# A convolution and MLP block on one core: features made between the units of the second projection, the last residual moved into the MLP, own tiles for passing loads, chunk loads by groups, another end

## The chip, the core and the metric

One core of a Trainium2 chip runs the whole kernel. TensorE (PE) multiplies; VectorE (DVE), ScalarE (ACT) and GpSimd (POOL) work on rows; SyncE (SP) issues DMAs, and so do POOL's and ACT's own queues. The metric is device time in microseconds (us) of one execution.

## The reference

One layer over 2048 tokens of width 1024. Its mixer is a short gated convolution, followed by a squared-ReLU MLP. Both parts have a root mean square norm ahead and behind.

```
a = modulate(rmsnorm(x, g_pre), shift1, scale1)
b, c, v = split(a @ sc_w_in, 3)
y = (b * depthwise_conv3(c * v, sc_conv)) @ sc_w_out
h = x + gate1 * rmsnorm(y, g_post)
m = modulate(rmsnorm(h, g_pre_ff), shift2, scale2)
f = square(relu(m @ w_in)) @ w_out          # w_in 1024x4096, w_out 4096x1024
out = h + gate2 * rmsnorm(f, g_post_ff)
```

The six rows of shifts, scales and gates come from silu(c) @ ada_w + ada_b.

## The kernel before

**Numbers.** All tensors are float32. Each operand of a large product is kept as a high and a low part of a shorter type (F32R), made by a cast on ScalarE and a subtraction on VectorE (`split`, L135), and each product is three matmuls of 128x128 by 128x512 (high by high, high by low, low by high). Features lie on the partitions, tokens along the free axis, 512 to a block; there are four blocks q = 0 to 3, and two pairs of blocks s = 0, 1. A tile of SBUF is [128, 2, 512] float32, 512 KB.

**Stages.** `conv_in(q)` multiplies by w_sci and gates; `conv_out(q)` (L312) multiplies by w_sco. It has 8 units j of 24 matmuls; behind each unit ScalarE copies the sums out of PSUM (y[j], L320), squares them (`ssy.add`), and behind all of them come the norm's rows (`rows`, L183), then the residual: x is loaded again (xr, L325), scaled y is added to it (L328, L329), the result goes to DRAM (h_buf, on POOL's queue, L331), and its squares give the rows of the next norm (rh). After conv_in(3) come m_of(0), conv_out(2) and conv_out(3). `m_of(s)` (L335) makes the MLP's input for a pair: for each of 8 k it loads h (hm, SP's queue), scales it on VectorE (L342), takes the high part on ScalarE (L343) and the low part on VectorE (L344). For each s there follow 16 steps of `hidden` (four chunks ch of the 4096 inner features, kp = 0 to 3; four groups of 24 matmuls each, then ReLU and square). The second MLP product is one level of a seven-product scheme for 2x2 blocks (`PRODUCTS`, L33), so `features` (L351) makes 7 tiles of sums and differences per hidden step and SP writes them to DRAM (h_store). Then come 16 units of `product` (L442), each 7 products m0 to m6 of 12 matmuls, adding into f tiles; the unit's first-time results are copied by ScalarE (L459), the others added by VectorE (L461). Each chunk needs 28 h tiles, loaded on POOL's queue (`load_hidden`, L393, issue at L400), for four units. `finish(s)` (L497) takes the norm of f, scales it, adds h and stores the output: for s = 0 in steps beside the hidden steps of s = 1, for s = 1 at the end.

**Order.** A scheduler (Tile) orders each engine's instructions ahead of the run by priority, which is the order in which the program emits them, except inside `tc.high_priority()`. Tiles of one tag are a ring: in the instruction list of this kernel, buffers of a tag are handed out in the order in which the program first writes its tiles, so a tile emitted later gets its buffer after all those emitted ahead of it. The tag ts has 41 tiles and serves nearly everything: y, m, hm, xr, h, f, e. The weights have tags of their own (wf 4 tiles raw, wr 7 split). Each waiting instruction holds what stands behind it on its engine or queue.

Of the kernel before, what the change touches and what calls it, by code (L numbers as in the profile page):

```python
# [9 lines left out]
F32 = mybir.dt.float32  # L10
# [5 lines left out]
D = 1024  # L16
# [23 lines left out]
def conv_block_kernel(ctx: ExitStack, tc: tile.TileContext, xt, c, cols, ada, w_first, w_sci, w_sco, w_in, w_out,  # L40
# [12 lines left out]
    def pair(name, tag="ts", dtype=F32):  # L53
        return sbuf([P, 2, TB], dtype, tag, bufs[tag], name)
# [50 lines left out]
    xt0 = [load(xt[0, i], f"xt0_{i}") for i in range(KT // 2)]  # L105
    cols_sb = const.tile([P, 13, KT], F32, name="cols_sb")
    nc.sync.dma_start(cols_sb, cols)
    gain_sb, adab_sb, convw_sb = cols_sb[:, 0:4], cols_sb[:, 4:10], cols_sb[:, 10:13]
# [200 lines left out]
                next(background, None)  # L309
            gate(q, j, *ps)  # L310

    def conv_out(q):  # L312

        g = [parts.pop((q, k)) for k in range(KT)]
        y, ssy = y_tiles(f"y{q}"), RootMean(f"ry{q}")
        for j in range(KT):
            w = load_weights(w_sco[j], f"wo{q}_{j}")
            ps = acc_bank(f"y{q}_{j}_ps")
            project(w, g, ps)
            nc.scalar.copy(y[j], ps)  # L320
            ssy.add(y[j])
        r = ssy.rows()
        ssh = RootMean(f"rh{q}")
        for i in range(KT // 2):
            xr = load(xt[q, i], f"xr{q}_{i}")  # L325
            for s in range(2):
                j = 2 * i + s
                nc.vector.scalar_tensor_tensor(y[j], y[j], G2[:, j:j + 1], r, op0=ALU.mult, op1=ALU.mult)  # L328
                nc.vector.tensor_add(xr[:, s], y[j], xr[:, s])  # L329
                ssh.add(xr[:, s])  # L330
                nc.gpsimd.dma_start(h_buf[q // 2][j][:, q % 2], xr[:, s])  # L331
        nc.gpsimd.dma_start(r_buf[q // 2][:, q % 2], ssh.rows())


    def m_of(s):  # L335

        r = load(r_buf[s], f"r2_{s}")
        res = []
# [7 lines left out]
        return res  # L346
# [4 lines left out]
    def features(y, name, to):  # L351

        y0, y2, y3 = y
        y1 = pair(f"{name}_y1")
# [31 lines left out]
    def one(res, name, t):  # L386
        res[name] = t[:, 0], t[:, 1]

    def two(res, names, tiles):
        for i, n in enumerate(names):  # L390
            res[n] = tuple(t[:, i] for t in tiles)

    def load_hidden(s, ch):  # L393

        tiles = [[None] * 7 for _ in range(KP)]
        for group in ((0,), (1, 2), (3, 4), (5, 6)):
            for kp in range(KP):
                for i in group:
                    t = tiles[kp][i] = pair(f"h{kp}_{i}", "ts", F32R)
                    nc.gpsimd.dma_start(t, h_store[s][ch][kp][i].bitcast(F32R))  # L400
        sets = []
        for x in tiles:
            res = {}
            one(res, "11", x[0])
            for i, names in enumerate((("T1", "T2"), ("21", "T3"), ("22", "T4"))):
                two(res, names, x[1 + 2 * i:3 + 2 * i])
            sets.append(res)
        return sets

    def lone(src, name, tag):  # L410
        t = pair(name, tag, F32R)
# [53 lines left out]
    class PairRootMean:  # L465
# [3 lines left out]
            self.name, self.acc, self.eps = name, None, EPS * D / P  # L469

        def add(self, x):
            sq = pair(f"{self.name}_sq")
            nc.scalar.activation(sq, x, AF.Square)
            if self.acc is None:
                self.acc = sq
            elif self.eps:
                nc.vector.scalar_tensor_tensor(self.acc, sq, self.eps, self.acc, op0=ALU.add, op1=ALU.add)
                self.eps = 0
            else:
                nc.vector.tensor_add(self.acc, self.acc, sq)  # L480

        def rows(self):
# [9 lines left out]
                nc.vector.scalar_tensor_tensor(r[:, i], v[:, i], 1.5, r[:, i], op0=ALU.add, op1=ALU.mult)  # L492
            return r

    f_buf = [dram_pair(f"fb{k}") for k in range(KT)]

    def finish(s, f, ss):  # L497
        r = ss.rows()
        for k in range(KT):
            h = load(h_buf[s][k], f"hr{s}_{k}")  # L500
            t = f[k] if s else load(f_buf[k], f"fr{k}")
            nc.vector.scalar_tensor_tensor(t, t, G5[:, k:k + 1], r, op0=ALU.mult, op1=ALU.mult)
            nc.vector.tensor_add(h, t, h)
            nc.sync.dma_start(out[s, k], h)
            yield


    def x_rows(q):
        ss = RootMean(f"rx{q}")
        for i in range(KT // 2):  # L510
            t = load(xt[q, i], f"xs{q}_{i}")
            for h in range(2):
                ss.add(t[:, h])
        return ss.rows()

    def a_of(q, r):
        res = []
        for i in range(KT // 2):
            t = load(xt[q, i], f"xt{q}_{i}")
# [3 lines left out]
        return res  # L523

    later = {}
    background = (s for m in (2, 3, 4, 5) for s in mod_rest(m))
# [33 lines left out]
    for q in range(1, NB):  # L560
        a = a1
        conv_in(q, a, range(4))
        if q < NB - 1:
            r = x_rows(q + 1)
        conv_in(q, a, range(4, 8))
        if q < NB - 1:
            a1 = a_of(q + 1, r)
        else:
            for j in range(KT):
                gate_split(q, j)  # L570
            later["m"] = m_of(0)
        for _ in background:
            pass
        conv_out(q - 1)
    conv_out(NB - 1)

    def run_makers(makers, i, then):
        def between(m):
            if m == 1 and then:
# [7 lines left out]
    rest = iter(())  # L587
    for s in range(NS):
        for ch in range(NCH):
            for kp in range(KP):  # L590
                if s and (ch, kp) == (0, 2):
                    rest = finish(0, f, ss)
                hidden(s, ch, kp, later["m"])
                if (ch, kp) > (1, 0):
                    next(rest, None)
        for _ in rest:
            pass
        units = [(ch, jp) for ch in range(NCH) for jp in range(KP)]
        ws = [{} for _ in units]
# [4 lines left out]
        later["h"] = load_hidden(s, 0)  # L604
        f, ss = [pair(f"f{s}_{j}") for j in range(KT)], PairRootMean(f"rf{s}")

        def fetch():
            if ch < NCH - 1:
                later["h"] = load_hidden(s, ch + 1)
            elif s < NS - 1:  # L610
                later["m"] = m_of(s + 1)

        for i, (ch, jp) in enumerate(units):
            h = later["h"]
            js = jp, jp + KP
            e = [f[j] for j in js]
            product(ws[i], h, e, f"f{s}_{ch}_{jp}", ch > 0, run_makers(makers, i, fetch if jp == KP - 1 else None))
            if ch == NCH - 1:
                for j in js:
                    ss.add(f[j])  # L620
                    if s == 0:
                        nc.sync.dma_start(f_buf[j], f[j])
    for _ in finish(NS - 1, f, ss):
        pass


_INS = ["xt", "c", "cols", "ada", "w_first", "w_sci", "w_sco", "w_in", "w_out"]

# [47 lines left out]
```

## Time and profile before

| what | us |
|---|---|
| median of three runs | 2176.29 (2174.86 to 2179.14) |
| the profiled execution | 2179.44 |
| its span (first to last instruction) | 2177.7 |
| PE busy in it | 2057.7 |
| last matmul of the last product starts | 2142.24 |

The profiled execution is one of its own, not one of the three. Its span leaves out what lies before the first and after the last instruction. The page's mean granted clock of PE over the span is 0.973 of full speed (2.4 GHz). A line such as `PE y_ps L153 <- ACT y L320` says that PE waited, ahead of the matmuls of line 153 into y_ps, for ScalarE's instruction of line 320; "x" counts instructions.

### The profile page before, as it was taken

To read this page: it belongs to the slowest core of one execution; us is meant where nothing else is said; L and a number is where in the kernel's file an instruction comes from. 1 tells how busy PE (TensorE), PEld (TensorE's weight loads), DVE (VectorE), ACT (ScalarE), POOL (GpSimd) and SP (SyncE) were. 2 spreads that over 40 slices of the span, in tenths; PEclk is the share of its full clock that TensorE was granted. 3 is DMA by queue.
4 is the path that set the end of the run, shared out by engine and by line. 5 is a ranking of instruction groups with operands and counts; after the bars stand their busy time and mean duration, and the time that the engine had idled before them with its cause. 6 is when DMAs were issued, how large, how long until landed. Compare 5 with 4: busy or idle time off the path is not lost.

```text
span 2177.7 us, 23307 instructions
## 1 busy us (share of the span) xinstructions
PE 2057.7 (94%) x8880; PEld 1683.0 (77%) x8880; DVE 1257.4 (58%) x1691; ACT 784.1 (36%) x1026; POOL 158.2 (7%) x272
## 2 busy tenths in 40 slices
PE   6799999999999789999998999998999999999993
PEld 3587888888888567888886888886888887788882
DVE  6768765865756666343444466575455554455666
ACT  3233334334433435444443212134444444221221
POOL 2000000000000000000012211200000002112100
PEclk7999999999999899999999999999999999999997
DMA  6565633433424347555579756754658789779533
GB/s 223 183 213 200 204 136 136 172 132 136 171 100 145 125 140 263 224 211 224 212 260 377 274 182 249 270 181 157 261 215 297 282 296 352 247 272 317 187 133 154
DMA packets 127696, 463.48 MB, mean 213 GB/s; under 512 B 14561, under 2 KB 14561, under 8 KB 127585
## 3 DMA queue, kind: packets, MB, share of 16 engines
q1 hardware_dynamic: 92448, 335.11, 42.7%
q0 software_dynamic: 35136, 126.89, 16.3%
q8 instruction: 69, 1.13, 0.2%
q14 instruction: 43, 0.34, 0.0%
HBM read 322.49 MB, written 139.46 MB: 212 GB/s over the span
## 4 chain that ended last, share of the span: by engine, by line
PE 83%; DMA 6%; DVE 4%; issue 3%; ACT 1%; POOL 1%; SPq 0%; DVEq 0%; POOLq 0%; ACTq 0%
PE hid L153 29%; PE c L153 20%; PE f_a L454 14%; PE y_ps L153 8%; PE f_b L454 7%; PE f_c L454 3%; DMA hs<-h_lo 1%; PE c L552 1%; DMA ada<-in_ada_dram 1%; DMA adar<-in_ada_dram 1%; DMA hm<-hb 1%; DMA h<-hs 1%; POOL h L400 1%; DMA xr<-in_xt_dram 1%; DVE ada L230 0%
## 5 line engine op out<-in xcount | busy, mean ns | idle before, releaser
L153 PE MATMUL c<-a_parts,wc_hi 128*128 128x512 f32 x1440 | 444.6, 390 | 0.7 <-ACT a_parts L219 0.7
L153 PE MATMUL hid<-m_hi,wi_hi 128*128 128x512 f32 x1024 | 395.2, 392 | 8.9 <-ACT m_hi L343 7.8
L153 PE MATMUL hid<-m_lo,wi_hi 128*128 128x512 f32 x1024 | 399.6, 390 | 0.0
L153 PE MATMUL hid<-m_hi,wi_lo 128*128 128x512 f32 x1024 | 399.4, 390 | 0.0
L153 PEld LDWEIGHTS c<-a_parts,wc_hi 128*128 128x128 f32 x1440 | 271.1, 188 | 57.7 <-ACT a_parts L219 1.1
L153 PE MATMUL c<-a_parts,wc_lo 128*128 128x512 f32 x720 | 280.7, 390 | 3.4 <-DVE wc_lo L137 3.4
L137 DVE TENSOR_TENSOR wi_lo<-wi,wi_hi 128x1024 fp32r<-128x1024 f32 x64 | 78.3, 1224 | 286.1 <-PE hid L153 280.6
L153 PEld LDWEIGHTS hid<-m_hi,wi_hi 128*128 128x128 f32 x1024 | 193.4, 189 | 51.3 <-ACT m_hi L343 9.5
L153 PEld LDWEIGHTS hid<-m_lo,wi_hi 128*128 128x128 f32 x1024 | 193.1, 189 | 40.3
L153 PEld LDWEIGHTS hid<-m_hi,wi_lo 128*128 128x128 f32 x1024 | 192.9, 188 | 40.2
L400 POOL DMA_DIRECT2D h<-hs x224 | 121.2, 541 | 1119.9 <-DMA hs<-h_lo 411.6
L153 PE MATMUL y_ps<-gs,wo_hi 128*128 128x512 f32 x512 | 160.4, 395 | 17.2 <-ACT y L320 17.2
L454 PE MATMUL f_a<-h,wf_s_hi 128*128 128x512 f32 x512 | 163.4, 394 | 10.7 <-ACT f L459 10.7
L454 PE MATMUL f_b<-h,wf_s_hi 128*128 128x512 f32 x512 | 166.8, 394 | 1.4 <-DMA h<-hs 1.1
L153 PEld LDWEIGHTS c<-a_parts,wc_lo 128*128 128x128 f32 x720 | 135.5, 188 | 31.9 <-DVE wc_lo L137 3.9
L137 DVE TENSOR_TENSOR wc_lo<-wc_raw,wc_hi 128x1024 fp32r<-128x1024 f32 x90 | 109.9, 1222 | 82.0 <-PE c L153 47.8
L381 ACT ACTIVATE e<-hid 128x512 f32<-128x512 f32 x128 | 75.2, 596 | 227.4 <-PE hid L153 227.4
L137 DVE TENSOR_TENSOR wf_s_lo<-wf_xs,wf_s_hi 128x1024 fp32r<-128x1024 f32 x64 | 78.3, 1224 | 96.3 <-PE f_a L454 42.3
L136 ACT CAST wc_hi<-wc_raw 128x1024 fp32r<-128x1024 f32 x90 | 94.7, 1053 | 107.1 <-issue 62.0
L153 PEld LDWEIGHTS y_ps<-gs,wo_hi 128*128 128x128 f32 x512 | 97.6, 191 | 38.6 <-ACT y L320 18.2
L136 ACT CAST wf_s_hi<-wf_xs 128x1024 fp32r<-128x1024 f32 x64 | 67.4, 1054 | 156.2 <-PE f_a L454 117.9
L454 PEld LDWEIGHTS f_a<-h,wf_s_hi 128*128 128x128 f32 x512 | 97.4, 190 | 31.8 <-ACT f L459 11.6
(180 smaller groups left out, 2916.9 us busy)
## 6 DMA issues: line engine op xcount, KB each, us to landing
h<-hs POOLq DMA_DIRECT2D x224, 512.0 KB, 9.9
hs<-h_hi SPq DMA_DIRECT2D x96, 512.0 KB, 4.5
hs<-h_lo SPq DMA_DIRECT2D x96, 512.0 KB, 5.6
wc_raw<-in_w_sci_dram SPq DMA_DIRECT2D x90, 512.0 KB, 3.3
wi<-in_w_in_dram SPq DMA_DIRECT2D x64, 512.0 KB, 4.0
wf_x<-in_w_out_dram SPq DMA_DIRECT2D x64, 512.0 KB, 4.9
adar<-in_ada_dram SPq DMA_DIRECT2D x32, 512.0 KB, 3.4
wo_raw<-in_w_sco_dram SPq DMA_DIRECT2D x32, 512.0 KB, 3.2
```

Of the source, the lines that this page charges most:

```text
L136: nc.scalar.copy(dst_hi, src)
L137: eng.tensor_sub(dst_lo, src, dst_hi.bitcast(F32))
L153: nc.tensor.matmul(ps, l, r, start=first and i == 0, stop=last and i == 2)
L381: nc.scalar.activation(e[0][:, q] if i == 0 else e[1 + q][:, 0], ps, AF.Relu)
L400: nc.gpsimd.dma_start(t, h_store[s][ch][kp][i].bitcast(F32R))
L454: nc.tensor.matmul(ps, l[:, cs], r, start=new and kp == 0 and n == 0, stop=kp == KP - 1 and n == 2, skip_group_check=True)
L552: nc.tensor.matmul(ps[i], l, m, start=k == 0 and t == 0, stop=k == KT - 1 and t == 2)
```

## The change

- **m_of(0) in steps.** m_of is a generator with one step for each k. For s = 0 it no longer stands ahead of conv_out(2): one step follows every second unit of conv_out(2), and the other four alternate with the steps of conv_out(2)'s residual between the units of conv_out(3). The low part of k is emitted one step later (`low_part`). The copies y[j] are emitted in high priority.
- **The last residual later.** conv_out is a generator that ends in the steps of `residual`: rows, four loads of xr with their sums, rows of h. Those of conv_out(3) now follow the hidden steps of s = 0 from (0, 1) on, one behind each.
- **Own tiles.** A tag x of 4 tiles serves xt0, xs, xt, xr, hm, hr, fr, the tile y1 of `features`, and the squares of f; ts goes from 41 to 37.
- **Chunk loads by groups.** `load_hidden` is a generator: 4 tiles for product m0, then 8 for m1 and m2, 8 for m3 and m4, 8 for m5 and m6. For the first chunk of a pair the last two groups are emitted behind m0 and m1 of its first unit; for later chunks all are emitted at once.
- **Another end.** For s = 1, `last` stands in place of the last unit's `ss.add` and of `finish`: squares by halves, three float32 matmuls of the sums and the two last squares, one half after the other; three of the eight k are scaled by G5 on ScalarE and multiplied and added on POOL in halves, five are done on VectorE in halves, with the order on these two engines as written, and 256 KB stores on ACT's and SP's queues.

```diff
-    bufs = {"ts": 41, "wf": 4, "wr": 7}
+    bufs = {"ts": 37, "x": 4, "wf": 4, "wr": 7}
...
-            nc.scalar.copy(y[j], ps)
+            with tc.high_priority():
+                nc.scalar.copy(y[j], ps)
             ssy.add(y[j])
+            if j % every == every - 1:
+                next(beside, None)
+        return residual(q, y, ssy)
+
+    def residual(q, y, ssy):
         r = ssy.rows()
+        yield
...
-    def m_of(s):
+    def m_of(s, res):
...
-            v = load(h_buf[s][k], f"hm{s}_{k}")
+            v = load(h_buf[s][k], f"hm{s}_{k}", "x")
...
-            nc.vector.scalar_tensor_tensor(lo, v, sh2[:, k:k + 1], hi.bitcast(F32), op0=ALU.add, op1=ALU.subtract)
+            if late:
+                low_part(*late)
+            late = lo, v, k, hi
...
-    def load_hidden(s, ch):
+    def load_hidden(s, ch, sets):
...
+        for group, names in (((0,), "11"), ((1, 2), ("T1", "T2")), ((3, 4), ("21", "T3")), ((5, 6), ("22", "T4"))):
...
+            yield
...
+    def last(f, js, ss):
...
+        order = [k for k in range(KT) if k not in js] + list(js)
+        shared, own = order[:KT - ts], order[KT - ts:]
+        for i in range(2):
+            for j, t in zip(js, parts[1:]):
+                nc.scalar.activation(t[:, i], f[j][:, i], AF.Square)
+            ps = tp_bank(f"rl_ps{i}")
+            for n, t in enumerate(parts):
+                nc.tensor.matmul(ps, onesf, t[:, i], start=n == 0, stop=n == len(parts) - 1)
+            nc.scalar.activation(r[:, i], ps, AF.Abs_reciprocal_sqrt, scale=1.0 / D)
...
+        for t, k in zip(gain, shared):
+            nc.scalar.activation(t, f[k], AF.Identity, scale=G5[:, k:k + 1])
+        with tc.manual_schedule(engines={mybir.EngineType.DVE, mybir.EngineType.Pool}):
+            for i in range(2):
+                for t, k in zip(gain, shared):
+                    nc.gpsimd.tensor_mul(t[:, i], t[:, i], r[:, i])
+                    nc.gpsimd.tensor_add(h[k][:, i], t[:, i], h[k][:, i])
+                    nc.scalar.dma_start(out[s, k, :, i], h[k][:, i])
+                for k in own:
...
+                    nc.vector.tensor_add(h[k][:, i], f[k][:, i], h[k][:, i])
+                    nc.sync.dma_start(out[s, k, :, i], h[k][:, i])
...
-            later["m"] = m_of(0)
...
-        conv_out(q - 1)
-    conv_out(NB - 1)
+        if q < NB - 1:
+            for _ in conv_out(q - 1):
+                pass
+    later["m"] = []
+    beside = m_of(0, later["m"])
+    rest = conv_out(NB - 2, beside, 2)
+    beside = alternate(rest, beside)
+    rest = conv_out(NB - 1, beside)
+
+    for _ in beside:
+        pass
...
-                if (ch, kp) > (1, 0):
+                if (ch, kp) > (0, 0):
                     next(rest, None)
```

## Rows read from the trace of the kernel before

**Rows 1.** The page's head and its part 1: busy time of each engine.
```profile
span 2177.7 us, 23307 instructions
...
PE 2057.7 (94%) x8880; PEld 1683.0 (77%) x8880; DVE 1257.4 (58%) x1691; ACT 784.1 (36%) x1026; POOL 158.2 (7%) x272
```

**Rows 2.** PE's waits on other engines: total us, times, longest us.
```profile
PE y_ps L153 <- ACT y L320: 17.2, 2, 16.0
...
PE f_a L454 <- ACT f L459: 10.7, 2, 5.4
...
PE hid L153 <- ACT m_hi L343: 7.8, 4, 3.0
...
PE rh_ps L189 <- ACT rh_parts L136: 7.7, 2, 6.7
```

**Rows 3.** Stretches: us; busy of PE, PEld, DVE, ACT, POOL; clock; DMA share; GB/s.
```profile
900.00:1000.00 100.00, 100.00 (x443) 82.78 (x442) 42.42 (x48) 46.08 (x61) 0.00 (x0) 1.00 0.54 205
...
677.00:710.00 33.00, 33.00 (x147) 27.32 (x146) 23.30 (x24) 15.56 (x20) 0.00 (x0) 1.00 0.52 190
...
710.00:732.00 22.00, 5.97 (x19) 4.46 (x18) 13.48 (x13) 11.62 (x17) 0.00 (x0) 0.61 0.25 96
...
732.00:770.00 38.00, 38.00 (x169) 31.45 (x168) 24.12 (x31) 13.14 (x18) 2.18 (x4) 1.00 0.47 156
...
770.00:787.00 17.00, 9.13 (x30) 6.46 (x29) 10.59 (x16) 10.19 (x19) 2.71 (x5) 0.70 0.51 163
...
825.00:833.00 8.00, 5.52 (x23) 3.79 (x22) 5.45 (x8) 4.78 (x9) 1.08 (x2) 1.00 0.22 85
...
1147.00:1190.00 43.00, 36.59 (x145) 28.02 (x144) 17.45 (x23) 13.15 (x19) 11.37 (x21) 0.92 1.11 410
...
1300.00:1340.00 40.00, 40.00 (x178) 32.97 (x177) 20.52 (x28) 7.25 (x8) 11.19 (x21) 1.00 1.00 360
...
1455.00:1500.00 45.00, 37.23 (x141) 28.96 (x140) 24.00 (x23) 10.87 (x10) 0.00 (x0) 0.89 0.50 178
```

**Rows 4.** ScalarE's timeline around 725 us: start, us, line, tile, [idle before, releaser].
```profile
724.86 1.15 ACT L343 ACTIVATE m_hi<-hm,mods 128x1024 fp32r<-128x1024 f32 x1 [2.61 <-DVE hm L342]
...
725.91 1.05 ACT L320 COPY y<-y_ps 128x512 f32<-128x512 f32 x2
```

**Rows 5.** All instructions by line and shape, the scaling in m_of.
```profile
L342 DVE SCALAR_TENSOR_TENSOR hm<-hm,mods,r 128x1024 f32<-128x1024 f32 x16 | 20.5, 1280 | 9.8 <-DMA hm<-hb 9.8
```

**Rows 6.** Timelines of ScalarE, then of POOL, in the first products.
```profile
1154.70 0.57 ACT L459 COPY f<-f_a 128x512 f32<-128x512 f32 x1
...
1180.29 0.54 POOL L400 DMA_DIRECT2D h<-hs  x1 [0.74 <-DMA h<-hs]
```

**Rows 7.** SP's timeline around 1487 us: DMA issues.
```profile
1487.39 1.33 SPq L78 DMA_DIRECT2D hm<-hb  x3
```

**Rows 8.** Timelines of VectorE, then of SP, at the end.
```profile
2142.67 0.69 DVE L461 TENSOR_TENSOR f<-f_a,f 128x512 f32<-128x512 f32 x1 [3.11 <-PE f_a L454]
...
2153.35 9.66 DVE L502 SCALAR_TENSOR_TENSOR f<-f,mods,rf_r 128x1024 f32<-128x1024 f32 x8
...
2162.93 9.16 DVE L503 TENSOR_TENSOR hr<-f,hr 128x1024 f32<-128x1024 f32 x8
...
2164.17 8.28 SPq L504 DMA_DIRECT2D out_dram<-hr  x8
```

**Rows 9.** Timelines of VectorE (four rows), then of POOL, in the start stage.
```profile
11.21 0.69 DVE L537 SCALAR_TENSOR_TENSOR rx<-rx 128x512 f32<-128x512 f32 x1 [0.35 <-ACT rx L534]
...
12.61 2.25 DVE L537 SCALAR_TENSOR_TENSOR rx<-rx 128x512 f32<-128x512 f32 x1
...
29.93 0.22 DVE L238 SCALAR_TENSOR_TENSOR mods<-mods,sb,cols_sb 128x1 f32<-128x1 f32 x1
...
54.88 1.84 DVE L238 SCALAR_TENSOR_TENSOR mods<-mods,sb,cols_sb 128x1 f32<-128x1 f32 x1
...
54.88 1.83 POOL L137 TENSOR_TENSOR w_lo<-w_raw,w_hi 128x768 fp32r<-128x768 f32 x1 [7.34 <-PE c L552]
```

More of the change, by code (lines that the diff above doesn't have):

```diff
@@ L104, in conv_block_kernel @@
     nc.sync.dma_start(c_sb, bass.AP(tensor=c.tensor, offset=c.offset, ap=[[0, P], [1, D]]))
-    xt0 = [load(xt[0, i], f"xt0_{i}") for i in range(KT // 2)]
+    xt0 = [load(xt[0, i], f"xt0_{i}", "x") for i in range(KT // 2)]
     cols_sb = const.tile([P, 13, KT], F32, name="cols_sb")
@@ L310, in conv_in, with conv_out @@
             gate(q, j, *ps)
-    def conv_out(q):
+    def conv_out(q, beside=iter(()), every=1):
         g = [parts.pop((q, k)) for k in range(KT)]
@@ L343, in m_of, with low_part @@
             nc.scalar.activation(hi, v, AF.Identity, bias=sh2[:, k:k + 1])
[L344 removed]
+            if late:
+                low_part(*late)
+            late = lo, v, k, hi
             res.append((hi, lo))
[L346 removed]
+            if k == KT - 1:
+                low_part(*late)
+            yield
+    def low_part(lo, v, k, hi):
+        nc.vector.scalar_tensor_tensor(lo, v, sh2[:, k:k + 1], hi.bitcast(F32), op0=ALU.add, op1=ALU.subtract)
     h_store = [[[[dram_pair(f"hs{s}_{ch}_{kp}_{i}") for i in range(7)] for kp in range(KP)] for ch in range(NCH)]
@@ L353, in features @@
         y0, y2, y3 = y
-        y1 = pair(f"{name}_y1")
+        y1 = pair(f"{name}_y1", "x")
         nc.vector.tensor_sub(y1[:, 0], y0[:, 1], y0[:, 0])
@@ L391, in two @@
             res[n] = tuple(t[:, i] for t in tiles)
-    def load_hidden(s, ch):
-        tiles = [[None] * 7 for _ in range(KP)]
-        for group in ((0,), (1, 2), (3, 4), (5, 6)):
+    def load_hidden(s, ch, sets):
+        sets += [{} for _ in range(KP)]
+        for group, names in (((0,), "11"), ((1, 2), ("T1", "T2")), ((3, 4), ("21", "T3")), ((5, 6), ("22", "T4"))):
             for kp in range(KP):
+                tiles = []
                 for i in group:
-                    t = tiles[kp][i] = pair(f"h{kp}_{i}", "ts", F32R)
+                    t = pair(f"h{kp}_{i}", "ts", F32R)
                     nc.gpsimd.dma_start(t, h_store[s][ch][kp][i].bitcast(F32R))
[L401 to L408, printed above, removed]
+                    tiles.append(t)
+                if len(group) == 1:
+                    one(sets[kp], names, tiles[0])
+                else:
+                    two(sets[kp], names, tiles)
+            yield
     def lone(src, name, tag):
@@ L471, in add @@
         def add(self, x):
-            sq = pair(f"{self.name}_sq")
+            sq = pair(f"{self.name}_sq", "x")
             nc.scalar.activation(sq, x, AF.Square)
@@ L493, in rows @@
             return r
+    def last(f, js, ss):
+        s, ts = NS - 1, 5
+        h = [load(h_buf[s][k], f"hl_{k}") for k in range(KT)]
+        parts = [ss.acc] + [pair(f"sl_{j}", "x") for j in js]
+        r, v = pair("rl_r"), pair("rl_v")
+        gain = [pair(f"gl_{k}") for k in range(ts, KT)]
+        order = [k for k in range(KT) if k not in js] + list(js)
[7 more added lines that the diff above has]
+            nc.scalar.activation(r[:, i], ps, AF.Abs_reciprocal_sqrt, scale=1.0 / D)
+            nc.vector.scalar_tensor_tensor(v[:, i], ps, -0.5 / D, r[:, i], op0=ALU.mult, op1=ALU.mult)
+            nc.vector.tensor_mul(v[:, i], v[:, i], r[:, i])
+            nc.vector.scalar_tensor_tensor(r[:, i], v[:, i], 1.5, r[:, i], op0=ALU.add, op1=ALU.mult)
+        for t, k in zip(gain, shared):
[7 more added lines that the diff above has]
+                for k in own:
+                    nc.vector.scalar_tensor_tensor(f[k][:, i], f[k][:, i], G5[:, k:k + 1], r[:, i], op0=ALU.mult,
+                                                   op1=ALU.mult)
+                    nc.vector.tensor_add(h[k][:, i], f[k][:, i], h[k][:, i])
+                    nc.sync.dma_start(out[s, k, :, i], h[k][:, i])
     f_buf = [dram_pair(f"fb{k}") for k in range(KT)]
@@ L510, in x_rows @@
         for i in range(KT // 2):
-            t = load(xt[q, i], f"xs{q}_{i}")
+            t = load(xt[q, i], f"xs{q}_{i}", "x")
             for h in range(2):
@@ L518, in a_of @@
         for i in range(KT // 2):
-            t = load(xt[q, i], f"xt{q}_{i}")
+            t = load(xt[q, i], f"xt{q}_{i}", "x")
             for h in range(2):
@@ L523, in a_of, with alternate @@
         return res
+    def alternate(*its):
+        its = list(its)
+        while its:
+            it = its.pop(0)
+            try:
+                next(it)
+            except StopIteration:
+                continue
+            its.append(it)
+            yield
     later = {}
@@ L570, in conv_block_kernel, with run_makers @@
                 gate_split(q, j)
-            later["m"] = m_of(0)
         for _ in background:
             pass
-        conv_out(q - 1)
-    conv_out(NB - 1)
-    def run_makers(makers, i, then):
+        if q < NB - 1:
[8 more added lines that the diff above has]
+        pass
+    def run_makers(makers, i, then, loading):
         def between(m):
+            if m in (0, 1):
+                next(loading, None)
             if m == 1 and then:
@@ L603, in conv_block_kernel @@
         next(makers[1])
-        later["h"] = load_hidden(s, 0)
+        later["h"] = []
+        loading = load_hidden(s, 0, later["h"])
+        next(loading)
+        next(loading)
         f, ss = [pair(f"f{s}_{j}") for j in range(KT)], PairRootMean(f"rf{s}")
@@ L608, in fetch @@
             if ch < NCH - 1:
-                later["h"] = load_hidden(s, ch + 1)
+                later["h"] = []
+                for _ in load_hidden(s, ch + 1, later["h"]):
+                    pass
             elif s < NS - 1:
-                later["m"] = m_of(s + 1)
+                later["m"] = []
+                for _ in m_of(s + 1, later["m"]):
+                    pass
         for i, (ch, jp) in enumerate(units):
@@ L616, in conv_block_kernel @@
             e = [f[j] for j in js]
-            product(ws[i], h, e, f"f{s}_{ch}_{jp}", ch > 0, run_makers(makers, i, fetch if jp == KP - 1 else None))
+            product(ws[i], h, e, f"f{s}_{ch}_{jp}", ch > 0, run_makers(makers, i, fetch if jp == KP - 1 else None, loading))
             if ch == NCH - 1:
                 for j in js:
-                    ss.add(f[j])
                     if s == 0:
+                        ss.add(f[j])
                         nc.sync.dma_start(f_buf[j], f[j])
-    for _ in finish(NS - 1, f, ss):
-        pass
+                    elif jp < KP - 1:
+                        ss.add(f[j])
+                if s and jp == KP - 1:
+                    last(f, js, ss)
 _INS = ["xt", "c", "cols", "ada", "w_first", "w_sci", "w_sco", "w_in", "w_out"]
```

9 lines of the change are left out of this document (4 added, 5 removed).

## The prediction

> **What bounds the kernel now.** I read the page's head and part 1 first. TensorE is busy for 94% of the span and no other engine for over 60% [rows 1], so time can only come from stretches in which TensorE stands, or runs slowly, and from the end. A stretch in which nothing disturbs it gives the pace: 443 matmuls in 100 us, 4.43 a us [rows 3]. The waits of TensorE on other engines then name the places [rows 2]: the y copies of ScalarE in conv_out (17.2 us), the f copies in the first products (10.7), the high parts of m (7.8) and the row sums of the residual (7.7). A wait is not the whole loss, since the clock falls behind it. So I take the stretches around these waits, and subtract from the width of each the time that its matmuls need at 4.43 a us [rows 3]:
>
> - 710 to 732: 22 − 19/4.43 = 17.7 us, granted clock 0.61 on average; 770 to 787: 17 − 30/4.43 = 10.2, clock 0.70; 825 to 833: 2.8. Together **A**, 30.7 us, around conv_out(2) and conv_out(3).
> - 1147 to 1190: 43 − 145/4.43 = 10.3, in the first product unit of s = 0, with the DMA engines at 410 GB/s. The pattern stands twice, once in each pair: **B**, 20.6 us.
> - 1455 to 1500: 45 − 141/4.43 = 13.2: **D**, where m_of(1) is made.
> - The end: the last product matmul starts at 2142.24 and ends at about T = 2142.6; the span ends at 2177.7. These 35.1 us are the **tail**, with VectorE at work nearly throughout [rows 8].
>
> The other losses, in the start stage above all, are touched by no edit.
>
> **The change part by part.** *Steps of m_of(0) (A).* Before, ScalarE's copies of y stand behind the m chain: the last such high part before the copies starts at 724.86 after 2.61 us of waiting for VectorE, and two copies follow at once at 725.91 [rows 4]. The 16 m tiles come ahead of the y tiles in the ring too. In the new order the y copies have priority and at most four steps of m are emitted ahead of the end of conv_out(2). What the m steps cost: 16 VectorE instructions, 8 to scale and 8 for the low parts, of about 1.28 us [rows 5], 20.5 us, the same as before but spread. Is there room? From 677 to 787 VectorE was busy for 23.3 + 13.5 + 24.1 + 10.6 = 71.5 us [rows 3]. The two conv_outs need 384/4.43 = 86.7 us. So VectorE goes to at most 82%, and it loses the last residual to the hidden steps as well, whose VectorE has 42 us in 100 busy [rows 3]; that is where this work is hidden. On SP's queue the xr and hm loads stand between w_sco's loads, on POOL's queue the residual's stores have nothing behind them until the chunk loads. The ring is the doubt: 16 split gate tiles, 8 y and 16 m make 40, more than 37, so the later m tiles wait for conv_out(2)'s gate tiles to come free. A row-sum matmul that stands in TensorE's order before its input is there can still hold it. The residual's rows cost 6.7 us at once [rows 2]; I leave about one such wait, 6, in place. **A: −25** (bounds: −31 if all goes, −12 if the 17.7 only halves and the rest of A shrinks by 3).
>
> *Chunk loads by groups (B).* The f copy, which ends the 5.4 us wait [rows 2], comes at 1154.70 [rows 6], behind the 28 h tiles in the ring. New, it stands behind 12. So that wait goes. But the loads set the next limit: one of 512 KB every 0.54 + 0.74 = 1.28 us [rows 6], at 410 GB/s [rows 3], and the last lands near 1186 whichever instruction comes before. With four fewer ts tiles, the first come two tiles later, 2.6 us. TensorE can bring forward only what its loaded tiles allow. I take a third of B back: **−7** (0 if the loads are the bound throughout, −14 if two thirds).
>
> *Fewer ts tiles (C).* In a product stage 28 h and 8 f tiles are held. Of 41, 5 were spare, of 37, 1 is: four loads at a chunk's boundary start only when an h tile comes free, 4 × 1.28 = 5.1 us later, at six boundaries, three in each pair. Before, TensorE ran at full pace across such a boundary with the DMA engines at share 1.00 (178 matmuls in the 40 us from 1300 [rows 3]). That shows that there was cover, not how much. In the first product of the new unit only four tiles are needed, so most of 5.1 is covered. **+2** (0 to 12, a third of 6 × 5.1).
>
> *Own tag for passing loads (D).* hm no longer stands behind the m tiles in the ring, so VectorE and ScalarE can start earlier; SP's queue stays in order, and three hm loads were issued together at 1487.39 [rows 7], behind a weight load. About half of D: **−6** (0 to −11).
>
> *The last residual beside w_in.* Its 16 VectorE instructions of 128x512, about 0.7 us each by the f sums [rows 8], 11 us, lie under four hidden steps at 42% of VectorE: 0. If that cover were gone, 11 us.
>
> *The other end.* Before: f's last sum at 2142.67, the final part from 2153.35 to 2172.1 (16 instructions in 9.66 + 9.16 = 18.8 us), and 5.6 us more to the span's end for the last stores [rows 8]. New: sum 0.7, square and float32 matmul and root about 2.3, three steps of 0.7, so the rows are ready near T + 5.8 in place of T + 10.7: −4.8. Then VectorE does 20 instructions of 128x512, half of 1.18 at least and 0.69 at most each [rows 8], 12.7 in all. POOL does 12. Its one known shape, 128x768, takes 1.83 us [rows 9], so by size 1.22, with some fixed cost 1.28: 15.4. Whether the two run side by side is the question. In the start stage VectorE's 128x512 instruction with two SBUF operands takes 2.25 us beside POOL where it takes 0.69 alone, and a tiny one takes 1.84 beside a POOL instruction of 1.83 and 0.22 alone [rows 9]: they took turns. So I take their sum, 28.1 in place of 18.8: +9.3. Smaller last stores give back about 1.5. **+3** (−9 if they overlap fully: 15.4 − 18.8 − 4.8 − 1; +6 if turns cost a little each).
>
> *y1 and the squares in tag x, xs and xt in tag x:* the conv_in stages ran without loss at these loads; 0 (−3 to +3).
>
> Sum: −25 − 7 + 2 − 6 + 3 = −33. The profiled execution took 2179.4, 3.1 above the median of 2176.3. −33 from the median gives 2143; I put **2142.5**, rounding for A's larger half.
>
> **Rivals.**
>
> 1. *Loads become the bound.* The chunk loads start later and the first unit of a pair waits for them just as long: B gives 0 in place of −7, C costs +12 in place of +2. For it: the 410 GB/s beside a 10 us loss [rows 3]. Against: full pace at share 1.00. Time: 2142.5 + 17 = **2159.5**. The Trainium skill (SBUF — State Buffer, the summary of rules for kernel authors) gives about 358 GB/s for transfers between HBM and SBUF. By that figure a 512 KB load would take an estimated 1.46 us, and 28 of them 5 us longer; the trace has 410 and does not agree.
>
> 2. *The m steps still hold the y copies*, so that the change doesn't do what it says: the ring of 37 is short, m tiles take the tiles that y of conv_out(3) needs, and the 17.7 us stay. For it: 40 tiles wanted of 37. Against: half the gate tiles are free by then. Time: 2142.5 + 17.7 = **2160**.
>
> 3. *The end overlaps.* VectorE and POOL run side by side, and the tail gives −9 in place of +3. Time **2130.5**. Against: the start rows. The Trainium skill (SBUF — State Buffer, Who interferes with whom) says that a VectorE instruction with two SBUF inputs and a GpSimd instruction that reads SBUF exclude each other for its whole length; that is what the start rows show, and it would keep the tail at the sum of both.
>
> 4. *Slower: late chunk loads at every boundary.* With one spare tile each of six boundaries waits 5.1 us, and each wait lowers the clock as in 1147 to 1190, where the mean of 0.92 over 43 us is 3.4 us lost [rows 3]: 6 × 8.5 = 51 in place of 2. Time 2142.5 + 49 = **2191**. It decides the sign from (33 + 2)/6 = 5.8 us a boundary. Against: full pace at the boundary before.
>
> **How the numbers follow.** The forecast has 0.50 (its own range 2131 to 2154, from A's and D's bounds), rival 1 0.18, rival 2 0.12, rival 3 0.11, rival 4 0.09. A range from 2126 to 2166 leaves out rival 4, a part of rival 3's lower half and the combination of rivals 1 and 2, about 0.2 together. A change of 0.2%, 4 us, is about what a measurement of this kernel can tell from none. All but rival 4 are faster by more; of rival 4, 0.02 lies within 4 us and 0.07 above. Faster 0.91, same 0.02, slower 0.07.
>
> **What would show it.** A: the wait of TensorE for the y copies falls under 3 us and the clock stays full around 710 to 730; if a wait of 16 us remains, rival 2. B: the wait for the f copy goes, and a wait of f_a or f_b for h's DMA takes its place, larger than 1 us; above 8 us in each pair, rival 1. C: TensorE waits for h's DMA at later boundaries, under 1 us each; 5 us each, rival 4. D: the waits for m_hi fall under half of 7.8. Tail: the rows ready within 6 us of the last product matmul, then VectorE's 0.69 us instructions stretched to about 1.9 beside POOL; if they stay at 0.69, rival 3. The prediction is wrong if the time is above 2172, or if it comes out right with A and the tail both off in opposite directions.

## The result, and the profile after

The changed kernel takes 2141.65 us in the median of three executions (2138.97 to 2143.33) where the kernel before takes 2177.68: ratio 0.9835 (95% interval 0.9815 to 0.9854), 36.0 us less. One more execution, with a granted clock of TensorE of 0.555 on average and 3499.64 us, is left out of this. A second measurement gave 2141.25 against 2179.73, ratio 0.982 (0.9806 to 0.9835), 38.5 us less. The forecast was 2142.5. The profile read here is that of the second measurement; the profiled execution took 2138.82 us.

The page's head and its part 1, of the changed kernel:

```profile
span 2136.7 us, 23360 instructions
...
PE 2048.2 (96%) x8888; PEld 1674.8 (78%) x8888; DVE 1256.7 (59%) x1692; ACT 783.1 (37%) x1030; POOL 176.8 (8%) x284
```

The span is 41.0 us shorter than in [rows 1], a little more than the medians differ, since this execution lies 2.4 us below its median and that of before 3.1 above. The other engines are busy as long as before, except POOL with 18.6 us more, its part of the new end. TensorE's waits in the changed kernel, the counterpart of [rows 2]:

```profile
PE f_a L468 <- ACT f L473: 9.0, 2, 4.5
PEld f_c L468 <- DMA h<-hs: 9.4, 10, 1.8
PE f_c L468 <- DMA h<-hs: 5.5, 7, 1.4
...
PE f_a L468 <- ACT wf L136: 2.0, 8, 0.3
```

The waits for the y copies, for the high parts of m and for the residual's row sums have left TensorE's list. The wait for the f copy is nearly what it was (9.0 in place of 10.7), and behind it stand new waits for h's DMA, all of the longer ones in the first product unit of a pair. The stretches, after:

```profile
195.00:217.00 22.00, 22.00 (x99) 18.23 (x98) 15.57 (x31) 7.34 (x9) 0.00 (x0) 1.00 0.61 198
...
690.00:800.00 110.00, 110.00 (x486) 91.09 (x486) 68.18 (x81) 54.30 (x76) 4.87 (x9) 1.00 0.50 170
1107.00:1153.00 46.00, 36.95 (x144) 26.90 (x143) 18.17 (x23) 14.25 (x20) 10.79 (x20) 0.96 1.02 372
1300.00:1340.00 40.00, 39.74 (x176) 32.50 (x175) 26.21 (x35) 8.14 (x10) 3.79 (x8) 1.00 0.35 110
1421.00:1466.00 45.00, 44.39 (x194) 35.84 (x193) 33.26 (x32) 22.82 (x26) 0.00 (x0) 1.00 0.54 187
...
1778.00:1824.00 46.00, 38.31 (x147) 28.28 (x146) 18.86 (x24) 14.14 (x20) 10.78 (x20) 0.93 1.01 375
```

and two stretches of before that the prediction had not shown, one in the input stage, one in the first unit of the second pair:

```profile
195.00:217.00 22.00, 17.86 (x71) 13.99 (x70) 19.05 (x34) 7.64 (x11) 0.00 (x0) 0.92 0.51 178
...
1825.00:1871.00 46.00, 39.79 (x159) 31.10 (x158) 20.31 (x27) 14.37 (x20) 11.62 (x22) 0.93 1.10 407
```

With the prediction's own reckoning (width less matmuls at 4.43 a us) the ledger is:

| place | lost before | lost after | difference | forecast |
|---|---|---|---|---|
| A, the two conv_outs | 30.7 | 110 − 486/4.43 = 0.3 | −30.4 | −25 |
| B, first product units of both pairs | 10.3 + 10.1 = 20.4 | 13.5 + 12.8 = 26.3 | +5.9 | −7 |
| C, later chunk boundaries (one of them, from 1300) | 0 | 0.3 | about +1 for all six | +2 |
| D, m_of(1) | 13.2 | 45 − 194/4.43 = 1.2 | −12.0 | −6 |
| input stage, 195 to 217 | 22 − 71/4.43 = 6.0 | 0 | −6.0 | 0 |
| end | 1.0 + 35.1 = 36.1 | 3.4 + 35.7 = 39.1 | +3.0 | +3 |

In the last row the first summand lies ahead of the last product and is read below; the second is the time from the last product's end to the span's end. The sum of the differences is about −38.5 of the −41.0 between the two spans; the rest lies in smaller places. So the time came out as forecast, but two terms were too small (A and D), one was missing (the input stage) and one had the wrong sign (B).

The end of the changed kernel, VectorE's timeline:

```profile
2101.02 0.69 DVE L475 TENSOR_TENSOR f<-f_a,f 128x512 f32<-128x512 f32 x1 [5.51 <-PE f_a L468]
...
2107.35 0.75 DVE L537 SCALAR_TENSOR_TENSOR f<-f,mods,rl_r 128x512 f32<-128x512 f32 x1
2108.14 1.63 DVE L539 TENSOR_TENSOR hl<-f,hl 128x512 f32<-128x512 f32 x1
2109.69 1.75 DVE L537 SCALAR_TENSOR_TENSOR f<-f,mods,rl_r 128x512 f32<-128x512 f32 x1
...
2126.37 1.74 DVE L537 SCALAR_TENSOR_TENSOR f<-f,mods,rl_r 128x512 f32<-128x512 f32 x1
2128.15 0.69 DVE L539 TENSOR_TENSOR hl<-f,hl 128x512 f32<-128x512 f32 x1
...
2132.32 0.69 DVE L539 TENSOR_TENSOR hl<-f,hl 128x512 f32<-128x512 f32 x1
```

POOL's timeline, and TensorE's just ahead of the last product:

```profile
2107.49 1.73 POOL L533 TENSOR_TENSOR gl<-gl,rl_r 128x512 f32<-128x512 f32 x1 [66.90 <-DVE rl_r L527]
2109.30 1.59 POOL L534 TENSOR_TENSOR hl<-gl,hl 128x512 f32<-128x512 f32 x1
...
2125.98 1.59 POOL L534 TENSOR_TENSOR hl<-gl,hl 128x512 f32<-128x512 f32 x1
...
2094.62 1.02 PE L523 MATMUL rl_ps<-rf_sq,onesf 128*128 128x512 f32 x2
...
2097.19 1.02 PE L523 MATMUL rl_ps<-sl,onesf 128*128 128x512 f32 x2
2097.65 1.02 PE L468 MATMUL f_a<-h,wf_a_hi 128*128 128x512 f32 x2
```

Each of the 12 VectorE instructions that start while POOL works, from 2107.5 to 2127.6, takes 1.63 to 1.75 us; the first one after it takes 0.69 again. From the rows' end at 2107.35 to 2133.0 are 25.7 us for 20 VectorE and 12 POOL instructions. The last product's matmuls end at T = 2101.0 and the span at 2136.7: 35.7 us. And four float32 matmuls, the row sums of the squares known by then, stand ahead of the last product: eight records that start 0.43 us apart, 3.4 us. In the kernel before, TensorE stood at this place for 1.0 us and waited for VectorE:

```profile
2139.62 0.73 PE L454 MATMUL f_a<-h,wf_a_hi 128*128 128x512 f32 x2 [1.02 <-DVE f L461]
```

### The profile page after: what moved, and what is told of

Same layout as the page of the kernel before. It is cut to its first block, busy times and chain, and to the rows that moved or that the text cites. A ratio compares the mean times of both kernels' runs of the same rounds, so it can differ in the third digit from the quotient of the medians.

```text
span 3497.5 us, 23360 instructions
## 1 busy us (share of the span) xinstructions
PE 3433.9 (98%) x8888; PEld 1947.7 (56%) x8888; DVE 1268.9 (36%) x1692; ACT 784.9 (22%) x1030; POOL 177.3 (5%) x284
## 4 chain that ended last, share of the span: by engine, by line
PE 97%; DVE 2%; DMA 1%; ACT 0%; issue 0%; POOL 0%; SPq 0%; DVEq 0%; POOLq 0%
PE hid L153 34%; PE c L153 24%; PE f_a L468 17%; PE y_ps L153 8%; PE f_b L468 8%; PE f_c L468 4%; PE c L610 1%; DMA ada<-in_ada_dram 1%; DVE f L537 0%; DVE ada L230 0%; PE rl_ps L523 0%; DVE hl L539 0%; ACT h_hi L136 0%; DMA xt<-in_xt_dram 0%; DVE rx L595 0%
## 5 line engine op out<-in xcount | busy, mean ns | idle before, releaser
L153 PE MATMUL c<-a_parts,wc_hi 128*128 128x512 f32 x1440 | 692.1, 576 | 0.0
L153 PE MATMUL hid<-m_lo,wi_hi 128*128 128x512 f32 x1024 | 589.9, 576 | 0.0
L153 PE MATMUL hid<-m_hi,wi_lo 128*128 128x512 f32 x1024 | 589.5, 576 | 0.0
L153 PE MATMUL hid<-m_hi,wi_hi 128*128 128x512 f32 x1024 | 588.3, 576 | 0.0
L153 PE MATMUL c<-a_parts,wc_lo 128*128 128x512 f32 x720 | 414.4, 576 | 0.0
L468 PE MATMUL f_b<-h,wf_s_hi 128*128 128x512 f32 x512 | 257.3, 576 | 0.0
L468 PE MATMUL f_a<-h,wf_s_hi 128*128 128x512 f32 x512 | 252.2, 577 | 4.6 <-ACT f L473 4.6
L153 PE MATMUL y_ps<-gs,wo_hi 128*128 128x512 f32 x512 | 246.3, 576 | 0.0
L468 PEld LDWEIGHTS f_b<-h,wf_s_hi 128*128 128x128 f32 x512 | 113.0, 221 | 84.6 <-issue 49.6
L468 PE MATMUL f_a<-h,wf 128*128 128x512 f32 x384 | 158.5, 576 | 0.0
```

The source lines that it names most:

```text
L153: nc.tensor.matmul(ps, l, r, start=first and i == 0, stop=last and i == 2)
L468: nc.tensor.matmul(ps, l[:, cs], r, start=new and kp == 0 and n == 0, stop=kp == KP - 1 and n == 2, skip_group_check=True)
```

## The experiments

**The changed kernel again (e0_after).** No edit.

> The changed kernel itself, for a profile with TensorE at full clock. By the terms of the prediction: the wait for the y copies under 3 us, around conv_out about 6 us lost in place of 30.7; in the first product unit of each pair the wait for the f copy gone and 5 to 8 us still lost to the chunk's loads; around 1455 to 1500 about 7 us lost in place of 13.2; from the last product matmul to the span's end about 38 us in place of 35.1. By the rival that the end overlaps: about 26 us at the end, and then some other term is 12 us worse than forecast, since the time came out as summed.

2141.25 us (2138.82 to 2144.22), the profile above. A and D are better than expected (0.3 us lost in place of about 6, 1.2 in place of about 7), and so is the part behind the last product (35.7 us in place of 38). B is worse: the wait for the f copy is not gone.

**m_of(0) at once (e1_m_at_once).**

```diff
-    beside = m_of(0, later["m"])
-    rest = conv_out(NB - 2, beside, 2)
-    beside = alternate(rest, beside)
+    for _ in m_of(0, later["m"]):
+        pass
+    beside = conv_out(NB - 2)
     rest = conv_out(NB - 1, beside)
```

> The changed kernel with m_of(0) emitted at once ahead of conv_out(2) and conv_out(2)'s residual alone beside conv_out(3); the y copies keep their priority. If the order of tiles in the ring holds the copies (the theory): the wait for the y copies comes back with some 16 us, TensorE falls to half clock behind it, and the time is 18 to 28 us above the changed kernel. If the priority of the copies alone removes the wait: within 4 us of the changed kernel.

2144.61 us (2141.32 to 2148.68), 3.4 above the changed kernel measured beside it, ranges overlapping. The wait of 16 us does not come back, against the theory in the expectation. With the tag x in place the steps are not needed to remove it; the priority could still be.

**Normal priority, with steps and without (e8_no_priority, e8b_once_no_priority).** The first takes the `with tc.high_priority():` away from the y copies, the second does that and the edit above.

```diff
-            with tc.high_priority():
-                nc.scalar.copy(y[j], ps)
+            nc.scalar.copy(y[j], ps)
```

> The changed kernel with the y copies at normal priority, m_of(0) in steps. If the steps are enough by themselves: within 3 us of the changed kernel. If the priority is what removes the wait: the wait for the y copies comes back, and the time is 10 to 25 us above.

> The changed kernel with m_of(0) emitted at once ahead of conv_out(2) and the y copies at normal priority: both halves of the edit around conv_out undone, the tag x and the later residual kept. If steps and priority each suffice: the wait of 16 us comes back here, and the time is 18 to 28 us above the changed kernel. If the tag x, or the residual moved away, is what removed it: within 5 us of the changed kernel.

2140.41 us (2139.15 to 2141.88) and 2144.56 (2142.0 to 2146.84). With both halves of the edit undone, TensorE's waits for the y copies, and for a weight's cast in the hidden step behind them, are these:

```profile
PE y_ps L153 <- ACT y L320: 1.7, 1, 1.7
...
PE hid L153 <- ACT wi_hi L136: 1.5, 1, 1.5
```

The first was 17.2 us in [rows 2] and is 1.7 here. So with the tag x neither steps nor priority are needed to remove it. The steps are worth 3 to 4 us in the medians (4.2 between these two runs, whose ranges do not overlap), of which these two waits are 3.2.

**Only the priority, in the kernel before (b1_priority).** The same two lines, added to the kernel before.

> The kernel before with one edit, the y copies in high priority. If the order of instructions on ScalarE held the copies: 18 to 25 us below the kernel before. If the ring of tiles held them (the m tiles handed out ahead of the y tiles, as the prediction says): within 4 us of the kernel before, with the wait of 16 us still there.

2180.94 us against 2181.68, ratio 0.9998 (0.9985 to 1.0011): the same. TensorE's wait for the y copies is still there, and ScalarE's timeline, shifted by 0.3 us, is that of [rows 4]:

```profile
PE y_ps L153 <- ACT y L321: 17.4, 2, 16.2
...
725.17 1.15 ACT L344 ACTIVATE m_hi<-hm,mods 128x1024 fp32r<-128x1024 f32 x1 [2.61 <-DVE hm L343]
726.23 1.05 ACT L321 COPY y<-y_ps 128x512 f32<-128x512 f32 x2
```

The priority did not move the copies ahead of the m chain: they keep their place in ScalarE's order. That leaves the tiles that they write into, which the next run changes.

**Only the tags, in the kernel before (b2_tag_x).** The passing loads, y1 and the squares of f go to tag x, and nothing else changes (the h tiles of the end stay in ts).

```diff
-    bufs = {"ts": 41, "wf": 4, "wr": 7}
+    bufs = {"ts": 37, "x": 4, "wf": 4, "wr": 7}
...
-            v = load(h_buf[s][k], f"hm{s}_{k}")
+            v = load(h_buf[s][k], f"hm{s}_{k}", "x")
```

> The kernel before with one part of the change: the tag x of 4 tiles for the passing loads, the squares of f and y1, and ts at 37 (the h tiles of the end stay in ts). No steps, no priority, no grouped loads, old end, last residual where it was. If the passing loads in the ring of ts were what held the y copies, the high parts of m and the second norm of the input stage: the waits for y and for m_hi fall under 3 us, the stall near 200 us goes, and the time is 30 to 45 us below the kernel before, with the first product units 5 to 15 us worse than before. If the steps or the later residual are needed beside the tag: under 20 us below the kernel before.

2143.52 us (2140.74 to 2145.82) against 2178.49, ratio 0.9833 (0.9817 to 0.985): as much as the whole change, to within what can be told. TensorE's wait for the y copies, and the stretches:

```profile
PE y_ps L153 <- ACT y L320: 1.2, 1, 1.2
...
195.00:217.00 22.00, 22.00 (x98) 18.21 (x97) 15.97 (x29) 6.29 (x8) 0.00 (x0) 1.00 0.63 196
...
700.00:805.00 105.00, 101.35 (x436) 82.58 (x436) 72.77 (x97) 50.20 (x79) 9.78 (x18) 0.98 0.45 156
1116.00:1162.00 46.00, 35.34 (x145) 27.30 (x144) 17.03 (x22) 13.42 (x19) 10.82 (x20) 0.89 1.03 375
1429.00:1474.00 45.00, 44.35 (x194) 36.09 (x194) 33.01 (x33) 21.92 (x25) 0.00 (x0) 1.00 0.55 193
...
1787.00:1833.00 46.00, 36.25 (x148) 29.01 (x147) 17.77 (x23) 13.30 (x19) 10.82 (x20) 0.89 1.02 374
```

The stall of the input stage is gone. The conv_outs lose 105 − 436/4.43 = 6.6 us in place of 30.7, m_of(1) loses 1.2 as in the changed kernel, the first product units lose 13.3 and 12.6. What the steps and the later residual add to the tags is nearly all of that 6.6. The times are equal all the same because this run has the old end, which is cheaper by 4.9 us (see e2_old_end below).

**All loads at once (e4_loads_at_once).** Four groups emitted ahead of the first unit.

```diff
-        next(loading)
-        next(loading)
+        for _ in loading:
+            pass
```

> The changed kernel with all 28 loads of the first chunk emitted ahead of the first product unit, as before. If the ring of tiles held the f copy (the prediction's reason for B): the wait for the f copy of the first unit grows by 2 us or more per pair, and the time by 3 to 10 us. If the copy only stands behind the casts of the last hidden step's features on ScalarE, as the changed kernel's profile now suggests with a wait of 4.5 us that stayed: the wait stays at 4 to 6 us per pair and the time within 3 us of the changed kernel.

2144.68 us (2144.37 to 2144.93), 3.4 above the changed kernel's median in the second measurement. Against the kernel before, measured beside each, the ratios are 0.9833 and 0.982, which are not told apart. The waits and the stretches, then ScalarE's copy:

```profile
PE f_a L468 <- ACT f L473: 19.1, 2, 9.8
...
1107.00:1153.00 46.00, 36.31 (x146) 28.73 (x145) 17.16 (x22) 13.41 (x19) 10.79 (x20) 0.89 1.02 379
1781.00:1829.00 48.00, 36.83 (x148) 28.21 (x147) 17.70 (x23) 13.41 (x19) 11.34 (x21) 0.89 1.00 363
...
1119.47 0.58 ACT L473 COPY f<-f_a 128x512 f32<-128x512 f32 x1 [4.12 <-DMA hs<-h]
```

The wait for the copy doubles to 9.8 in each pair, and ScalarE stands idle for 4.1 us ahead of it, so with 37 tiles the ring does hold the copy when all loads come first; with groups 4.5 remain. But the units lose 13.0 and 14.6 us, 27.6 together, against 26.3 with groups, and b2_tag_x, which has 37 tiles and no groups either, loses 25.9: with groups TensorE got the copy sooner and then waited for loads instead. Why 4.5 remain is on ScalarE's timeline, first of the changed kernel, then of the kernel before:

```profile
1112.30 1.99 ACT L136 CAST h_hi<-e 128x1024 fp32r<-128x1024 f32 x2
1114.19 0.57 ACT L473 COPY f<-f_a 128x512 f32<-128x512 f32 x1
...
1152.29 1.99 ACT L136 CAST h_hi<-e 128x1024 fp32r<-128x1024 f32 x2
1154.18 0.61 ACT L136 CAST wf<-wf_x 128x512 fp32r<-128x512 f32 x1
```

The f copy stands right behind the last hidden step's casts. It did so before, too: the copy at 1154.70 [rows 6] follows these casts without idle time of ScalarE.

**One tile fewer (e9_ts36).** `"ts": 36` in place of 37.

> The changed kernel with one ts tile fewer, 36, so that no tile is spare while 28 h and 8 f tiles are held. If the four tiles taken from ts are what made the first product unit of each pair 3.4 us worse than before: 1 to 2 us more lost in each pair here, and 2 to 6 us above the changed kernel. If the loads there are bound by the DMA rate alone: within 2 us. If each later chunk boundary had lost its last cover: 20 us or more above, with waits for h at all six.

2143.22 us (2139.79 to 2143.48), ratio 0.9827 (0.9809 to 0.9846); not told apart from the changed kernel by time. By the profile:

```profile
1109.00:1155.00 46.00, 37.45 (x144) 28.09 (x143) 18.03 (x23) 14.25 (x20) 10.82 (x20) 0.93 1.00 370
1780.00:1830.00 50.00, 40.65 (x152) 30.86 (x151) 19.78 (x25) 14.26 (x20) 11.37 (x21) 0.86 0.97 350
```

13.5 + 15.7 = 29.2 us lost in the first units, 2.9 more than with 37 tiles. At the later boundaries TensorE waits for no h tile, though no tile is spare.

**Another end (e2_old_end, e3_end_dve).** The first puts the end of before back, the second keeps the new one and gives POOL nothing (`s, ts = NS - 1, KT`).

```diff
-                    elif jp < KP - 1:
-                        ss.add(f[j])
-                if s and jp == KP - 1:
-                    last(f, js, ss)
+    for _ in finish(NS - 1, f, ss):
+        pass
```

> The changed kernel with the end of before (norm over whole tiles, all eight k on VectorE in tiles of 1024, 512 KB stores, h tiles from tag ts). If the new end costs 3 us, as the prediction's term for the tail: 3 us below the changed kernel, with 35 us from the last product matmul to the span's end. If VectorE and POOL overlap in the new end: 9 us above the changed kernel.

> The changed kernel with all eight k of the end on VectorE in halves, none on POOL. VectorE then does 32 instructions of 128x512, some 20 us from the rows on. If VectorE and POOL take turns in the changed kernel (28 us there): 7 us below the changed kernel. If they overlap (15.4 us there): 5 us above it.

2136.37 us (2135.47 to 2136.98) with the old end and 2137.67 (2135.2 to 2138.72) with VectorE alone, against 2141.25 (2138.82 to 2144.22) of the changed kernel measured beside them. VectorE's timeline in the second:

```profile
2107.82 0.75 DVE L537 SCALAR_TENSOR_TENSOR f<-f,mods,rl_r 128x512 f32<-128x512 f32 x1
2108.61 0.69 DVE L539 TENSOR_TENSOR hl<-f,hl 128x512 f32<-128x512 f32 x1
...
2129.44 0.69 DVE L539 TENSOR_TENSOR hl<-f,hl 128x512 f32<-128x512 f32 x1
```

32 instructions in 22.3 us, where 20 beside POOL's 12 took 25.7: moving three of eight k to POOL made the part 3.4 us longer. The expectation had 7 us, since it counted each POOL instruction with 1.28 us.

**A wide end (e11_end_wide), and with one tile more (e12_wide_ts38).** In the first, the square of the last unit's first f tile is added on VectorE, and all eight k are done on VectorE in whole tiles, the last in halves. The second adds `"ts": 38` and one buffer in place of two for the tag cb.

```diff
+            nc.vector.tensor_add(ss.acc[:, i], ss.acc[:, i], first[:, i])
...
+            for k in range(KT):
+                for c in ((slice(0, 2),) if k < KT - 1 else (slice(0, 1), slice(1, 2))):
+                    nc.vector.scalar_tensor_tensor(f[k][:, c], f[k][:, c], G5[:, k:k + 1], r[:, c], op0=ALU.mult,
+                                                   op1=ALU.mult)
+                    nc.vector.tensor_add(h[k][:, c], f[k][:, c], h[k][:, c])
```

> The changed kernel with another end: the square of the last unit's first f tile added on VectorE, so that two float32 matmuls a half remain, and all eight k on VectorE in tiles of 1024 (the last k in halves), none on POOL. If taking turns with POOL and the 128x512 instructions cost what the profiles show (3.3 and 3.4 us) and a third of the row sums' 3.3 us can be left out: 7 to 9 us below the changed kernel, 28 to 30 us from the last product matmul to the span's end. If the later first store takes it back: 3 us below, as with all on VectorE in halves.

> The same as the kernel with the wide end, with one ts tile more, 38, paid for by one buffer in place of two for b in the gate. If a spare ts tile is worth 1 to 2 us in each first unit: 2 to 4 us below the kernel with the wide end, unless the single buffer delays the gates of conv_in, which would show as waits of TensorE there. If the DMA rate alone binds: the same.

2134.48 us (2132.8 to 2135.53), ratio 0.9792 (0.9777 to 0.9807), and 2133.51 (2133.26 to 2134.35), ratio 0.9789 (0.9774 to 0.9803): both below the changed kernel (2141.25) and the kernel before (2178.49), and not told apart from each other. The first is 6.8 us below the changed kernel, a little less than the 7 to 9 expected. The wide end on VectorE:

```profile
2101.33 0.69 DVE L475 TENSOR_TENSOR f<-f_a,f 128x512 f32<-128x512 f32 x1 [3.76 <-PE f_a L468]
...
2107.66 1.28 DVE L530 SCALAR_TENSOR_TENSOR f<-f,mods,rl_r 128x1024 f32<-128x1024 f32 x1
...
2127.03 0.69 DVE L532 TENSOR_TENSOR hl<-f,hl 128x512 f32<-128x512 f32 x1
```

The last product ends at 2101.3 and the span at 2131.0: 29.7 us in place of 35.7. With 38 tiles the first units are these:

```profile
1111.00:1157.00 46.00, 38.69 (x148) 29.20 (x146) 18.97 (x24) 14.13 (x20) 10.83 (x20) 0.89 1.04 377
1783.00:1829.00 46.00, 39.04 (x154) 29.68 (x153) 20.40 (x26) 13.79 (x20) 10.83 (x20) 0.93 1.03 380
```

12.6 + 11.2 = 23.8 us lost, where the wide end with 37 tiles (e11_end_wide) loses 13.5 + 13.3 = 26.8.

## Why the prediction was right, and where it was wrong inside

**A: the place and about the size were right, but another edit does most of it than the one credited.** The prediction names two things that hold the copies, ScalarE's order behind the m chain and the ring of tiles, and gives the 25 us to "the new order", with priority and steps. b1_priority shows that priority alone does not change ScalarE's order, e8b_once_no_priority that with the tag x the stall stays away without steps and priority, b2_tag_x that the tags alone remove 24 of the 30.4 us. Whether the steps alone, with 41 tiles in ts and no tag x, would have removed it too was not tried. The count that the prediction made for the new ring should have been made for the old one: m_of(0)'s r, 8 hm and 16 m tiles with 16 gate tiles are 41, all of ts, so the y tiles, emitted after them, had to wait until the m chain gave tiles back. With hm in a tag of its own the same sum is 33 of 37. That count is from the code; the runs agree with it, but no run shows it by itself, and which of the loads in tag x mattered most was not tried. Rival 2, which feared the short ring, did not come. Beside the tags, the steps and the later residual are worth the remaining 6 us, not 25.

**B: the step that failed.** "So that wait goes" was wrong, and "I take a third of B back" had the wrong sign. The prediction put the wait of 5.4 us down to the 28 h tiles in the ring; but before, the copy followed casts on ScalarE with no idle time between, and those casts are still there. Emitting the loads by groups removes only the wait that the shorter ring adds (9.8 to 4.5 us at 37 tiles). And the prediction's own sentence, that the loads set the next limit, was the answer: the part of rival 1's mechanism that concerns B. Before, 12 loads had been issued and 8 had landed when the first product started, and the 28th landed 39.5 us after; in the changed kernel 9 and 4, and 42.9; with 36 tiles 8 and 4, and 43.0; with 38, 10 and 5, and 42.1 (counted over POOL's issues in the first pair). The loss in both first units follows: 20.4 us at 41 tiles (without groups), 23.8 at 38, 26.3 at 37, 29.2 at 36. So the four tiles that tag x took cost 5.9 us here, for which the prediction had 2.6 a pair in mind and then did not put it into the sum. By the landings, the price of 1.28 us a load held only for the last ten loads; in the changed kernel the 9th to the 18th land 2.6 us apart. The DMA engines' share in the window is 1.02 at 372 GB/s (before, 1.11 at 410), so the trace shows no slack in which late loads could catch up.

**C:** +2 was a little too much, and rival 4 did not appear. TensorE waits for no h tile at a later boundary, with one spare tile or with none (e9_ts36); what is lost there is a wait of 0.26 us for a weight's cast at each of the six, where before had it at two.

**D:** right in mechanism and too small. The prediction left half of the loss to the order of SP's queue; b2_tag_x shows that the tag alone leaves 1.2 us, so the queue order cost at most that once a tile was there.

**Input stage:** put at 0, because "the conv_in stages ran without loss". They did not: 195 to 217 lost 6.0 us. These are gone in the changed kernel and with the tags alone, which take x's loads for the next block out of ts there; so it was the tags, and by the same reasoning the ring.

**The end:** +3 forecast, +3.0 by the profile, +4.9 by the medians with the old end in its place. Four terms were off and cancelled: the part that VectorE and POOL share took 25.7 us, not 28.1, so that by subtraction a POOL instruction cost (25.7 − 20 × 0.69)/12 = 0.99 us, not 1.28; the float32 row sums cost 3.4 us on TensorE ahead of the last product, in place of a wait of 1.0, and the sum had nothing for those; the last stores gave back 1.9 (3.7 us behind the last instruction in place of 5.6), not 1.5; the rows came at T + 6.3, not T + 5.8. That VectorE and POOL take turns was right, and rival 3 is refuted. The Trainium skill (SBUF — State Buffer, Who interferes with whom) says that a VectorE instruction with two SBUF inputs contends with a GpSimd instruction that reads SBUF, and that the lock on the shared ports is exclusive; the 1.63 to 1.75 us in place of 0.69 agree with it.

**The number.** A and D came out 11 us better than forecast, the input stage 6, and B 13 worse. That 2142.5 was hit so closely is luck: these errors cancel in large part, and the number should not be read as a proof of the steps. The prediction had said that it would be wrong with A and the tail off in opposite directions. A was 5.4 us better; the tail was right by the profile and 1.9 worse by the medians, so that this sign is met in part, and the larger errors lay in places that it did not name.

## What to carry to other kernels

When instructions with short-lived tiles share a ring with long-lived ones, count the tiles that are emitted ahead of a critical write: if they fill the ring, that write can wait for their whole chain. Here a higher priority did not move it, and a small tag of their own for the passing loads did. A tile taken from a ring that prefetches has a price at the first use (here about 0.7 us a tile in each pair for the first four, 1.5 for the fifth), so look for both ends of the trade. Before an engine's wait is put down to a ring, see whether the instruction that ends it had idle time ahead of it; if not, the work ahead of it on its own engine holds it. And before work is shared with POOL at an end that VectorE bounds, see in the trace whether the two run side by side on that kind of operand: here three eighths of the work given away made it 3.4 us longer.

## What the runs showed of the hardware that was not expected

Beside VectorE instructions with two SBUF operands, POOL did 12 instructions of 128x512 float32 in 20.1 us, each in turn with one of VectorE: 1.67 us for the two, of which VectorE alone needs 0.69. The 0.99 us that remain for POOL are less than its size had suggested from 1.83 us for 128x768 [rows 9]; they are a difference, and no run here has such a POOL instruction alone. A float32 matmul of 128x512 stands in the trace as two records that start 0.43 us apart, 0.86 us together, where the split products' matmuls start 0.23 us apart at the same granted clock of 1.00: nearly four of them.
